# T sums of h in a second lane, z of the first half through DRAM, hi a unit ahead of lo

## The chip, the cores and the metric

The kernel runs on one core of one Trainium2 chip. The metric is the device time of one launch in microseconds. The median of three runs is 2718.05 us (2717.44 to 2718.52).

## What is computed

One residual block over 528 tokens (16 meta tokens and 512 of the sequence) of 2048 channels, in float32:

```
h = RMSNorm_pre(r);  z = h @ W_in + b_in      -> q, k, v, forget logits, pool input, two gates
m = sigmoid(g_attn) * (attention @ W_attn_o) + sigmoid(g_pool) * (pool @ W_pool_o)
r = r + RMSNorm_post(m @ W_out)
h = RMSNorm_pre(r)
a = causal_conv3(h @ W_up);  gate, val = split(a)          (11264 columns, 5632 each)
r = r + RMSNorm_post((gelu(gate) * val) @ W_down)
```

## The kernel before

**Layout and splitting.** Channels lie on the 128 partitions and tokens along the free axis. Every float32 product is made of three TensorE products of reduced-precision parts: each operand is split into hi (a cast by ScalarE, ACT) and lo (operand minus hi, by VectorE, DVE), and hi*hi, hi*lo and lo*hi are summed in PSUM.

**Weights.** They come from HBM in half tiles of 128x1024 ("units"), the loads on SP's queue. `load_next` fills `wraw` (six buffers), `convert_next` makes `whi` (L214, ACT) and then at once `wlo` (L215, DVE) in four buffers each. `weights` serves a tile of two units: when a tile begins it has the conversions up to two units past its own first two written out, and one more from its second half. Everything is issued in one order written out by hand: an engine executes its instructions in the order in which the Python emits them.

**Side work.** `Side` holds generators. `mm3` emits the matmuls of one k block and then calls `side.tick` with the time they are credited with (3 x 258 columns / 2330 = 0.332 for a half of the tokens). A generator that has yielded a number continues when that much was credited. `side.finish` emits all that is left at once.

**The stretch that the change touches.** The tokens are cut into two halves of 258 (with an overlap of two). The mixer's output projection (`mixer_out`, tile `pw`) first finishes half 0, then runs 12 tiles for half 1, about 1141 to 1215 us. Beside these 12 tiles goes `mixer_norm` of half 0. It reads the sum of squares (`rstd_from`: a matmul into `ps_rs`, then DVE and ACT steps, ending in the inverse root). Its first loop scales the projection (L814, DVE), adds the old residual (L818, POOL, with x loaded three steps ahead), stores it, squares it (L824, ACT) and adds up the squares (L816, DVE and POOL in turn); a second `rstd_from`; its second loop then makes h (L834, DVE), its hi (L836, ACT), stores h to DRAM and, one step later, makes its lo (L831, DVE). The numbers 2.2 and 2.0 (half 0), 1.8 and 1.5 (half 1) are the yields of the two loops. Then come the first six channel tiles of W_up for gate and value, once for half 0 and once for half 1 (`up_half`, tile `pu`, 12 tiles each); beside those of half 0 goes `mixer_norm` of half 1.

**Strassen-like pairs.** The other 38 channel tiles (`up_pair`) take seven products of 24 matmuls each in place of eight, over sums of weight blocks (S1 to S4, DVE) and sums of h blocks (T1 to T4). `sums_of_h` loads h from DRAM and makes the T's for each of eight k blocks: four DVE sums, two ACT casts, two DVE subtractions (L863 to L873). It is put into `side` when the second half phase starts, `combine` of a finished channel tile (convolution, gelu, product) is put ahead of it, and a `side.finish` ahead of the pairs emits what is left. In a pair, PSUM partial sums are copied by ACT to a `snap` tile (L914), and DVE adds a PSUM bank to that into `z`. All tiles of class F (activations) share 62 slots.

Of the kernel before, what the change touches and what calls it, by code (L numbers as in the profile page):

```python
# [32 lines left out]
LOOK = 3  # L33
# [19 lines left out]
EPS = 1e-6  # L53
NF = 62
NSP = 10
# [17 lines left out]
def block(ctx, tc, xT, win, wf, wao, wpw, wpo, wout, wup, wdn, consts, out):  # L73
# [50 lines left out]
    order += [("out", i) for i, _ in out_steps]  # L124
    NH = 6
    ups = lambda f0, f1: [("up", s * FT + f) for f in range(f0, f1) for s in (0, 1)]
    order += ups(0, NH) * 2
# [10 lines left out]
    for key in order:  # L138
# [10 lines left out]
    raws, ready, sums = {}, {}, {}  # L149
    at = {"load": 0, "conv": 0, "use": 0, "live": 0}  # L150
    NU = len(units)
# [24 lines left out]

    def unit_source(kind, n):

        if kind == "":
            return raw_of(n), lambda: drop(n)  # L180
        a11, a12, a21, a22 = (raw_of(n + i) for i in range(4))
        if kind == "11":
            return a11, lambda: None
        if kind == "12":
            return a12, lambda: None
        if kind == "22":
            return a22, lambda: drop(n + 3)
        if kind == "S3":
            def done():
                drop(n + 2)  # L190
                dve.tensor_tensor(a12, a12, sums["s2"], op=OP.subtract)
            return a21, done
        if kind == "S4":
            return a12, lambda: drop(n + 1)
        if kind == "S1":
            def done():
                dve.tensor_tensor(a21, a11, a21, op=OP.subtract)
                drop(n)
            return sums["s1"], done

        s1, s2 = (wp.tile([P, 1024], F32, name="wsum", tag="wsum", bufs=2) for _ in range(2))
        sums.update(s1=s1, s2=s2)
        dve.tensor_tensor(s1, a21, a22, op=OP.add)
        dve.tensor_tensor(s2, s1, a11, op=OP.subtract)  # L204
        return s2, lambda: None

    def convert_next(copy=act.copy):
        n = at["conv"]
        if n < NU - 8:
            kind, first = units[n]  # L210
            raw, done = unit_source(kind, first)
            hi = wp.tile([P, 1024], F32R, name="whi", tag="whi", bufs=HI)
            lo = wp.tile([P, 1024], F32R, name="wlo", tag="wlo", bufs=LO)
            copy(hi, raw)  # L214
            dve.tensor_tensor(lo, raw, f32(hi), op=OP.subtract)  # L215
            ready[n] = (hi, lo)
            done()
            at["conv"] += 1

    def prepare(n):  # L220
        while at["conv"] < min(NU - 8, n):
            convert_next()

    def weights(*key, ahead=1):

        n = at["use"]
        assert order[n] == key, (order[n], key)
        at["use"] += 1
        u = base[n]
        prepare(u + 2 + (2 if ahead else -1))  # L230
        if ahead:
            load_ahead()
        def w(t):
            if t >= 8 and ahead:
                prepare(u + 5)
                load_ahead()
            c = P * (t % 8)
            hi, lo = ready[u + t // 8]
            return hi[:, c:c + P], lo[:, c:c + P]
        return w  # L240

    def pair_weights(f):

        n = at["use"]
        assert order[n] == ("pair", f), (order[n], f)
        at["use"] += 1
        u = base[n]
        def unit(i):
            prepare(u + i + 1 + LOOK)
            load_ahead()  # L250
            hi, lo = ready[u + i]
            return lambda k: (hi[:, P * k:P * (k + 1)], lo[:, P * k:P * (k + 1)])
        return unit
# [41 lines left out]

    side = Side()

# [4 lines left out]
    def mm3(parts, nk, w, x, more=False):  # L302

        us = sum(3 * (xs.stop - xs.start) / 2330.0 for _, xs in parts)
        for k in range(nk):
            wh, wl = w(k)
            xh, xl = x(k)
            for j, (a, b) in enumerate(((wh, xh), (wh, xl), (wl, xh))):
                for po, xs in parts:
                    pe.matmul(po, a, b[:, xs], start=k == 0 and j == 0 and not more,  # L310
                              stop=k == nk - 1 and j == 2, skip_group_check=more)
            side.tick(us)


# [61 lines left out]
    for k in range(KT):  # L376
# [26 lines left out]
        if k == 7:  # L403
            convert_next()
    for k in range(KT - 3, KT):
# [359 lines left out]
    h_dram = dp.tile([2, KT, P, NA], F32, name="h_dram")  # L765
    act_dram = dp.tile([FT, P, SEQ], F32, name="act_dram")
    hb = [[], []]

# [3 lines left out]
    def mixer_out(i, es):  # L772
# [8 lines left out]
        for e, ps in zip(es, pss):  # L781
            if mix[e][i] is None:
                both = F("mix", n=2 * NA)
                mix[e][i & ~1], mix[e][i | 1] = both[:, :NA], both[:, NA:]
            act.copy(mix[e][i], ps)
            sq = F("sq2", n=NA)
# [6 lines left out]
    def mixer_norm(e, mix, acc, pace, pace2):  # L793
# [59 lines left out]

    def sums_of_h():

        for k in range(HK):
# [8 lines left out]
            h13, l13 = F("h13", F32R, 2 * NA), F("l13", F32R, 2 * NA)  # L865
# [3 lines left out]
            h24, l24 = F("h24", F32R, 2 * NA), F("l24", F32R, 2 * NA)  # L869
            act.copy(h24, t24)  # L870
            yield 1.5
            dve.tensor_tensor(l13, t13, f32(h13), op=OP.subtract)
            dve.tensor_tensor(l24, t24, f32(h24), op=OP.subtract)  # L873
            for name, h, l, j in (("T1", h13, l13, 0), ("T3", h13, l13, 1), ("T2", h24, l24, 0), ("T4", h24, l24, 1)):
                ts[name, k] = h[:, NA * j:NA * (j + 1)], l[:, NA * j:NA * (j + 1)]
            yield 1.5
# [28 lines left out]

    def up_half(e, m, z):
# [5 lines left out]
    def snap(src):  # L912
        t = sp.tile([P, NA], F32, name="snap", tag="snap", bufs=4)
        act.copy(t, src)  # L914
        return t

    def up_pair(f, late=None):
# [5 lines left out]
        def product(i, ps, block, more=False):  # L923
            mm3([(ps, slice(0, NA))], HK, unit(i), BLOCKS[block], more)

        product(0, a, "11")
# [12 lines left out]
        product(6, a, "T4", True)  # L939
        dve.tensor_tensor(zg[:, NA:NT], u2[:, 2:], c[:, 2:], op=OP.add)  # L940
        act.copy(zv[:, :NA], a)
        side.add(combine(zg, zv, f))

    zs = {}
    for e in range(2):
        if e == 1:
            side.finish()
            side.add(sums_of_h())
        for f in range(NH):
            for m in (f, FT + f):  # L950
                if e == 0:
                    zs[m] = F("z")
                up_half(e, m, zs[m])
            if e == 1:
                done = combine(zs.pop(f), zs.pop(FT + f), f)
                side.gens.insert(0, done) if side.gens else side.add(done)
    side.finish()

# [173 lines left out]
```

## Time and profile before

| | |
|---|---|
| median of three runs | 2718.05 us |
| the profiled execution | 2717.18 us, span 2715.4 us |
| mean granted TensorE clock | 0.983 |
| busy: PE, DVE, ACT, POOL | 97%, 61%, 38%, 5% of the span |

The profile page gives each engine's busy time, the span in 40 slices with the granted clock, the chain of waits that ended last and the costliest groups of instructions. Matmuls overlap in their pipeline, so PE's busy time alone doesn't tell its rate; the number of matmuls in a stretch does. PE is the TensorE matmul, PEld its weight load.

### The profile page before, as it was taken

The numbers are of one execution on the slowest core, as the hardware profiler recorded it, in microseconds if no ns is written. First come the engines' busy times: TensorE is split into PE (matmuls) and PEld (weight loads), VectorE is DVE, ScalarE is ACT, GpSimd is POOL, SyncE is SP. The second block draws the span as 40 slices with busy tenths as digits, with TensorE's granted clock in tenths as the row PEclk, the third lists the DMA queues.
The fourth block names the chain that finished last, engine by engine and source line by source line (L and its number), as shares of the span: only waits on it lengthen the run. The fifth ranks groups of instructions, "written<-read, shape, count | busy, mean of one in ns | idle before, by whom it ended". The sixth has DMA issues, their size and how long they took to land.

```text
span 2715.4 us, 46577 instructions
## 1 busy us (share of the span) xinstructions
PE 2622.0 (97%) x19669; PEld 2519.4 (93%) x19669; DVE 1652.6 (61%) x2144; ACT 1044.2 (38%) x1524; POOL 149.1 (5%) x204
## 2 busy tenths in 40 slices
PE   8999999999999999988969999999999999999995
PEld 8999999999999999988869999999999988888885
DVE  7655543223533334577688888888888845454557
ACT  4443342222232224444545455554554542222222
POOL 3000000000000000033000000000000000000003
PEclk9999999999999999998989999999999999999998
DMA  4322223332234323576643333333333343333323
GB/s 177 102 79 80 79 77 108 108 105 94 90 117 125 113 99 135 179 231 216 198 147 125 110 119 126 107 121 125 105 123 123 109 154 130 119 114 124 116 86 124
DMA packets 119377, 334.01 MB, mean 123 GB/s; under 512 B 13430, under 2 KB 38264, under 8 KB 119168
## 3 DMA queue, kind: packets, MB, share of 16 engines
q1 hardware_dynamic: 114944, 317.31, 35.4%
q0 software_dynamic: 4224, 13.72, 1.4%
q8 instruction: 154, 2.52, 0.4%
q14 instruction: 55, 0.45, 0.1%
HBM read 301.55 MB, written 29.43 MB: 122 GB/s over the span
## 4 chain that ended last, share of the span: by engine, by line
PE 89%; DVE 5%; issue 2%; ACT 2%; DMA 2%; POOL 0%; SPq 0%; DVEq 0%; ACTq 0%; POOLq 0%
PE pd L310 17%; PE pua L310 16%; PE puc L310 8%; PE pgp L310 7%; PE pga L310 7%; PE pw L310 6%; PE pu L310 6%; PE pub L310 4%; PE pv L310 3%; PE pao L310 3%; PE pk L310 3%; PE ppo L310 3%; PE pq L310 3%; ACT whi L214 1%; PE pa L589 1%
## 5 line engine op out<-in xcount | busy, mean ns | idle before, releaser
L215 DVE TENSOR_TENSOR wlo<-wraw,whi 128x1024 fp32r<-128x1024 f32 x536 | 659.4, 1232 | 417.5 <-ACT whi L214 416.9
L214 ACT CAST whi<-wraw 128x1024 fp32r<-128x1024 f32 x536 | 561.1, 1049 | 742.6 <-PE pd L310 227.9
L310 PE MATMUL pua<-h,whi 128*128 128x258 f32 x1520 | 370.2, 284 | 28.5 <-ACT snap L914 25.3
L310 PE MATMUL pua<-h,wlo 128*128 128x258 f32 x1216 | 345.6, 284 | 0.0
L310 PEld LDWEIGHTS pua<-h,whi 128*128 128x128 f32 x1520 | 267.6, 190 | 28.9 <-ACT snap L914 25.5
L310 PE MATMUL pua<-l,whi 128*128 128x258 f32 x912 | 259.1, 284 | 0.0
L310 PE MATMUL pd<-fh,wlo 128*128 128x512 f32 x640 | 252.2, 394 | 0.0
L310 PE MATMUL pd<-fh,whi 128*128 128x512 f32 x640 | 251.8, 393 | 0.0
L310 PE MATMUL pd<-fl,whi 128*128 128x512 f32 x640 | 251.7, 393 | 0.0
L310 PEld LDWEIGHTS pua<-h,wlo 128*128 128x128 f32 x1216 | 231.9, 191 | 0.0
L310 PE MATMUL puc<-h,whi 128*128 128x258 f32 x912 | 198.7, 284 | 0.0
L989 DVE TENSOR_TENSOR yacc<-yacc,pd 128x512 f32<-128x512 f32 x144 | 98.6, 685 | 145.1 <-PE pd L310 145.1
L310 PEld LDWEIGHTS pua<-l,whi 128*128 128x128 f32 x912 | 173.8, 191 | 0.0
L310 PE MATMUL puc<-h,wlo 128*128 128x258 f32 x608 | 172.4, 284 | 0.0
L310 PE MATMUL pu<-h,whi 128*128 128x258 f32 x768 | 149.9, 296 | 13.1 <-ACT sq L787 9.2
L310 PEld LDWEIGHTS puc<-h,whi 128*128 128x128 f32 x912 | 152.9, 190 | 0.0
L310 PEld LDWEIGHTS pd<-fl,whi 128*128 128x128 f32 x640 | 120.2, 188 | 28.2
L310 PEld LDWEIGHTS pd<-fh,wlo 128*128 128x128 f32 x640 | 120.2, 188 | 27.8
L310 PEld LDWEIGHTS pd<-fh,whi 128*128 128x128 f32 x640 | 120.2, 188 | 27.8
L310 PEld LDWEIGHTS pu<-h,whi 128*128 128x128 f32 x768 | 126.1, 200 | 16.0 <-ACT sq L787 9.4
L214 ACT CAST whi<-wsum 128x1024 fp32r<-128x1024 f32 x76 | 79.9, 1051 | 155.3 <-DVE wsum L204 155.3
L310 PE MATMUL pw<-ml,whi 128*128 128x258 f32 x512 | 136.1, 286 | 1.5 <-DVE ml L300 1.4
(316 smaller groups left out, 6109.1 us busy)
## 6 DMA issues: line engine op xcount, KB each, us to landing
wraw<-wup SPq DMA_DIRECT2D x200, 512.0 KB, 3.7
wraw<-win SPq DMA_DIRECT2D x128, 512.0 KB, 3.6
wraw<-wdn SPq DMA_DIRECT2D x88, 512.0 KB, 3.6
wraw<-wout SPq DMA_DIRECT2D x56, 512.0 KB, 3.9
act_dram<-cv POOLq DMA_DIRECT2D x44, 256.0 KB, 4.7
y<-act_dram SPq DMA_DIRECT2D x44, 256.0 KB, 4.9
wraw<-wao SPq DMA_DIRECT2D x16, 512.0 KB, 3.6
wraw<-wpo SPq DMA_DIRECT2D x16, 512.0 KB, 3.8
```

What stands on the lines that cost most here:

```text
L214: copy(hi, raw)
L215: dve.tensor_tensor(lo, raw, f32(hi), op=OP.subtract)
L310: pe.matmul(po, a, b[:, xs], start=k == 0 and j == 0 and not more, stop=k == nk - 1 and j == 2, skip_group_check=more)
L589: pe.matmul(pa[:, q0:], u, w[:, q0:], start=n == 0 and j == 0, stop=n == 4 and j == 2)
L989: dve.tensor_tensor(yacc[i], yacc[i], ps, op=OP.add)
```

## The change

- `NF` goes from 62 to 63 slots.
- The conversion of weights is cut into three steps with counters of their own: the sum or load (`make_source`), hi (`make_hi`) and lo (`make_lo`). In `weights`, lo is written out to one unit less far than before, hi one unit and sources two units ahead of lo. In pairs lo goes as far as before, hi isn't ahead, and a source is made right after the lo of the unit before it.
- `mixer_out` applies the post-norm's gain when it copies PSUM (an ACT activation with a scale); `mixer_norm` then multiplies by the inverse root alone. Its yields become 1.7 and 1.5 for both halves. In its second loop hi comes one step and lo two steps after h.
- `Side` exists twice; `mm3` ticks both. `sums_of_h` runs for k blocks 0 to 4 in the second lane beside `up_half` of half 1; blocks 5 to 7 are emitted after that phase, at once, ahead of the first pair. `combine` of the last half-phase tile is no longer finished ahead of the pairs.
- z of half 0 goes through DRAM: a POOL-issued store in the first half phase and an SP-issued load in the second, in place of 12 F tiles that stayed.
- In pairs, partial sums are copied by ACT straight into z and DVE adds in place; one ACT copy more per pair (`vr`).

```diff
-NF = 62
+NF = 63
...
+    def make_hi():
+        i = at["hi"]
+        while at["sum"] <= i:
+            make_source()
+        ready[i] = [wp.tile([P, 1024], F32R, name="whi", tag="whi", bufs=HI)]
+        act.copy(ready[i][0], sources[i])
+        at["hi"] += 1
+
+    def make_lo():
+        i = at["lo"]
+        while at["hi"] <= i:
+            make_hi()
+        lo = wp.tile([P, 1024], F32R, name="wlo", tag="wlo", bufs=LO)
+        dve.tensor_tensor(lo, sources.pop(i), f32(ready[i][0]), op=OP.subtract)
...
+    def prepare(n, ahead=1, ahead2=None):
+        n = min(n, NU - 8)
+        while at["lo"] < n:
+            make_lo()
+            for step, d, make in (("sum", 2 * ahead if ahead2 is None else ahead2, make_source), ("hi", ahead, make_hi)):
+                if at[step] < min(at["lo"] + d, NU - 8):
+                    make()
...
-        prepare(u + 2 + (2 if ahead else -1))
+        prepare(u + (LOOK if ahead else 1), ahead)
...
-                prepare(u + 5)
+                prepare(u + 1 + LOOK)
...
-            prepare(u + i + 1 + LOOK)
+            prepare(u + i + 1 + LOOK, 0, 1)
...
-    side = Side()
+    side, side2 = Side(), Side()
...
             side.tick(us)
+            side2.tick(us)
...
-            act.copy(mix[e][i], ps)
+            act.activation(mix[e][i], ps, AF.Identity, scale=col(C_G[1] + i))
...
-                dve.scalar_tensor_tensor(t, t, col(C_G[1] + i), rs1, op0=OP.mult, op1=OP.mult)
+                dve.tensor_tensor(t, t, rs1, op=OP.mult)
...
-        for i in range(KT + 1):
+        for i in range(KT + 2):
             yield pace2
-            if i:
-                hl = hb[e][i - 1]
-                dve.tensor_tensor(hl[:, NA:], mix[i - 1], f32(hl[:, :NA]), op=OP.subtract)
+            if i > 1:
+                hl = hb[e][i - 2]
+                dve.tensor_tensor(hl[:, NA:], mix[i - 2], f32(hl[:, :NA]), op=OP.subtract)
             if i < KT:
                 t = mix[i]
                 dve.scalar_tensor_tensor(t, t, col(C_G[2] + i), rs2, op0=OP.mult, op1=OP.mult)
+            if 1 <= i <= KT:
                 hl = F("h2", F32R, 2 * NA)
-                act.copy(hl[:, :NA], t)
-                nc.sync.dma_start(h_dram[e, i], t)
+                act.copy(hl[:, :NA], mix[i - 1])
+                nc.sync.dma_start(h_dram[e, i - 1], mix[i - 1])
                 hb[e].append(hl)
...
-            side.add(mixer_norm(0, mix[0], macc[0], 2.2, 2.0))
+            side.add(mixer_norm(0, mix[0], macc[0], 1.7, 1.5))
     side.finish()
-    side.add(mixer_norm(1, mix[1], macc[1], 1.8, 1.5))
+    side.add(mixer_norm(1, mix[1], macc[1], 1.7, 1.5))
...
-            yield 4.0
+            yield 3.0
...
+        z = F("z") if e else F("z0", n=NA)
+        if e:
+            nc.sync.dma_start(z[:, :NA], z_dram[n])
         mm3([(ps, slice(0, NA))], KT, w, lambda k: h_block(e, k))
-        act.copy(z[:, NA * e:NT], ps[:, 2 * e:]) if e else act.copy(z[:, :NA], ps)
+        if e:
+            act.copy(z[:, NA:NT], ps[:, 2:])
+        else:
+            act.copy(z, ps)
+            nc.gpsimd.dma_start(z_dram[n], z)
+        return z
...
         product(0, a, "11")
-        p1 = snap(a)
+        act.copy(gl, a)
         product(1, b, "21")
         product(2, a, "T2", True)
-        dve.tensor_tensor(zg[:, :NA], p1, b, op=OP.add)
-        u2 = snap(a)
+        act.copy(gr, a[:, 2:])
+        dve.tensor_tensor(gl, gl, b, op=OP.add)
         product(3, c, "T1")
-        p5 = snap(c)
+        act.copy(p5, c)
         product(4, a, "T3", True)
+        act.copy(vr, a[:, 2:])
         product(5, c, "22", True)
-        dve.tensor_tensor(zv[:, NA:NT], p5[:, 2:], a[:, 2:], op=OP.add)
+        dve.tensor_tensor(vr, vr, p5[:, 2:], op=OP.add)
         product(6, a, "T4", True)
...
         if e == 1:
             side.finish()
-            side.add(sums_of_h())
+            side2.add(sums_of_h(range(KE)))
...
-    side.finish()
+    side2.finish()
+    side2.add(sums_of_h(range(KE, HK)))
+    side2.finish()
```

## Rows read from the trace of the kernel before

**Rows 1.** The page: busy us, share of the span and instructions of each engine.
```profile
PE 2622.0 (97%) x19669; PEld 2519.4 (93%) x19669; DVE 1652.6 (61%) x2144; ACT 1044.2 (38%) x1524; POOL 149.1 (5%) x204
```
**Rows 2.** Busy time by stretch; after the stretch its length, x counts instructions.
```profile
core 0: us, PE busy (x) PEld busy (x) DVE busy (x) ACT busy (x) POOL busy (x), PEclk, DMA share, GB/s
...
1190.00:1200.00 10.00, 8.07 (x54) 7.84 (x53) 8.33 (x12) 4.09 (x10) 1.37 (x1) 0.83 0.67 230
...
1215.10:1240.00 24.90, 14.84 (x84) 13.35 (x83) 16.26 (x30) 10.80 (x22) 0.00 (x0) 0.73 0.48 152
1240.00:1270.00 30.00, 30.00 (x251) 30.00 (x250) 24.25 (x32) 13.88 (x26) 18.19 (x19) 1.00 0.87 272
1270.00:1285.00 15.00, 10.38 (x62) 9.77 (x62) 11.99 (x16) 7.21 (x12) 4.12 (x5) 0.77 0.67 213
1285.00:1325.00 40.00, 34.39 (x252) 32.42 (x251) 23.40 (x41) 16.97 (x30) 0.00 (x0) 0.94 0.54 172
1325.00:1335.00 10.00, 9.27 (x69) 9.06 (x68) 4.39 (x8) 4.40 (x7) 0.00 (x0) 0.89 0.48 159
1335.00:1389.80 54.80, 54.80 (x454) 54.80 (x453) 40.64 (x43) 32.70 (x44) 0.00 (x0) 1.00 0.66 216
...
1396.00:1421.00 25.00, 0.11 (x1) 0.11 (x1) 23.34 (x48) 9.92 (x16) 3.04 (x6) 0.56 0.39 127
1421.00:1441.00 20.00, 20.00 (x148) 20.00 (x149) 14.84 (x16) 9.06 (x12) 0.00 (x0) 0.87 0.32 106
1455.30:2143.10 687.80, 687.80 (x5714) 687.80 (x5713) 590.16 (x647) 349.21 (x476) 18.39 (x34) 1.00 0.35 118
```
**Rows 3.** PE's waits, 1130 to 1445 us: total us, times, longest.
```profile
PE pua L310 <- ACT snap L914: 25.3, 1, 25.3
```
**Rows 4.** PE's waits, 1421 to 2190 us.
```profile
PE pua L310 <- DVE z L938: 3.2, 1, 3.2
```
**Rows 5.** DVE in order of time, second loops: start, length, operation, [idle before <- releaser].
```profile
1231.40 0.43 DVE L831 TENSOR_TENSOR h<-mix,h 128x258 fp32r<-128x258 f32 x1 [0.47 <-ACT h L836]
...
1232.69 0.43 DVE L831 TENSOR_TENSOR h<-mix,h 128x258 fp32r<-128x258 f32 x1 [0.47 <-ACT h L836]
...
1315.08 1.23 DVE L215 TENSOR_TENSOR wlo<-wraw,whi 128x1024 fp32r<-128x1024 f32 x1 [1.69 <-ACT whi L214]
1316.22 0.42 DVE L831 TENSOR_TENSOR h<-mix,h 128x258 fp32r<-128x258 f32 x1
1316.56 0.48 DVE L834 SCALAR_TENSOR_TENSOR mix<-mix,cs,rs 128x258 f32<-128x258 f32 x1
```
**Rows 6.** DVE in order of time, the first loop of half 1.
```profile
1246.51 0.48 DVE L814 SCALAR_TENSOR_TENSOR mix<-mix,cs,rs 128x258 f32<-128x258 f32 x1
...
1273.64 0.95 DVE L814 SCALAR_TENSOR_TENSOR mix<-mix,cs,rs 128x258 f32<-128x258 f32 x1
```
**Rows 7.** Groups of DVE, 1242.4 to 1277.5 us: busy us, mean ns, idle before.
```profile
L215 DVE TENSOR_TENSOR wlo<-wraw,whi 128x1024 fp32r<-128x1024 f32 x13 | 17.1, 1312 | 7.4 <-ACT whi L214 7.4
```
**Rows 8.** POOL in order of time, the first loop of half 1.
```profile
1253.73 1.72 POOL L816 TENSOR_TENSOR acc<-acc,sq 128x258 f32<-128x258 f32 x1
...
1274.67 0.76 POOL L818 TENSOR_TENSOR mix<-mix,x 128x258 f32<-128x258 f32 x1 [0.36 <-DVE mix L814]
```
**Rows 9.** DMA issues, 1130 to 1430 us: count, KB each, median us to landing.
```profile
x<-xT SPq DMA_DIRECT2D x32, 129.0 KB, 5.0
```
**Rows 10.** DVE in order of time around the end of the half phases.
```profile
1387.78 1.23 DVE L204 TENSOR_TENSOR wsum<-wsum,wraw 128x1024 f32<-128x1024 f32 x1
...
1398.40 0.42 DVE L863 TENSOR_TENSOR t<-t 128x258 f32<-128x258 f32 x1
...
1401.50 0.42 DVE L863 TENSOR_TENSOR t<-t 128x258 f32<-128x258 f32 x1
```
**Rows 11.** ACT in order of time, in a pair.
```profile
1533.24 1.05 ACT L214 CAST whi<-wraw 128x1024 fp32r<-128x1024 f32 x1 [1.47 <-issue]
```
**Rows 12.** Groups of POOL, whole span: count, busy us, mean ns, idle before.
```profile
L903 POOL DMA_DIRECT2D act_dram<-cv x44 | 23.8, 542 | 897.8 <-DVE cv L902 897.6
```

More of the change, by code (lines that the diff above doesn't have):

```diff
@@ L125, in block @@
     NH = 6
+    KE = 5
     ups = lambda f0, f1: [("up", s * FT + f) for f in range(f0, f1) for s in (0, 1)]
@@ L148, in block @@
                 loads.append((srcs[key[0]](*key[1:]), c))
-    raws, ready, sums = {}, {}, {}
-    at = {"load": 0, "conv": 0, "use": 0, "live": 0}
+    raws, sources, ready, sums = {}, {}, {}, {}
+    at = {"load": 0, "sum": 0, "hi": 0, "lo": 0, "use": 0, "live": 0}
     NU = len(units)
@@ L175, in load_ahead, with make_source @@
             load_next()
-    def unit_source(kind, n):
+    def make_source():
+        i = at["sum"]
+        kind, n = units[i]
         if kind == "":
[L180 to L196, printed above, removed]
+            sources[i] = raw_of(n)
+        else:
+            a11, a12, a21, a22 = (raw_of(n + j) for j in range(4))
+            if kind == "S2":
+                for name in ("S1", "S2"):
+                    sums[name] = wp.tile([P, 1024], F32, name="wsum", tag="wsum", bufs=2)
+                dve.tensor_tensor(sums["S1"], a21, a22, op=OP.add)
+                dve.tensor_tensor(sums["S2"], sums["S1"], a11, op=OP.subtract)
+            elif kind == "S3":
@@ L197, in done @@
                 dve.tensor_tensor(a21, a11, a21, op=OP.subtract)
                 drop(n)
[L199 to L218, printed above, removed]
@@ L220, in prepare @@
-    def prepare(n):
-        while at["conv"] < min(NU - 8, n):
-            convert_next()
+            elif kind == "S4":
+                dve.tensor_tensor(a12, a12, sums["S2"], op=OP.subtract)
+            sources[i] = {"11": a11, "12": a12, "S3": a21, "S4": a12, "22": a22}.get(kind) or sums[kind]
+        at["sum"] += 1
+    def make_hi():
[5 more added lines that the diff above has]
+        at["hi"] += 1
@@ new lines, in make_lo @@
+    def make_lo():
[4 more added lines that the diff above has]
+        dve.tensor_tensor(lo, sources.pop(i), f32(ready[i][0]), op=OP.subtract)
+        ready[i].append(lo)
+        kind, n = units[i]
+        last = {"": 0, "S3": 2, "S4": 1, "22": 3}.get(kind)
+        if last is not None:
+            drop(n + last)
+        at["lo"] += 1
+    def prepare(n, ahead=1, ahead2=None):
[5 more added lines that the diff above has]
+                    make()
@@ L403, in block @@
         if k == 7:
-            convert_next()
+            make_lo()
     for k in range(KT - 3, KT):
@@ L766, in block @@
     act_dram = dp.tile([FT, P, SEQ], F32, name="act_dram")
+    z_dram = dp.tile([2 * NH, P, NA], F32, name="z_dram")
     hb = [[], []]
@@ L852, in block, with sums_of_h @@
     ts = {}
-    def sums_of_h():
-        for k in range(HK):
+    def sums_of_h(ks):
+        for k in ks:
             t13, t24 = F("t13", n=2 * NA), F("t24", n=2 * NA)
@@ L868, in sums_of_h @@
             dve.tensor_tensor(b21, b21, b22, op=OP.subtract)
-            h24, l24 = F("h24", F32R, 2 * NA), F("l24", F32R, 2 * NA)
             act.copy(h24, t24)
[L871 to L875, printed above, removed]
+            yield 2.0
+            for names, h, t in ((("T1", "T3"), h13, t13), (("T2", "T4"), h24, t24)):
+                lo = F("lt", F32R, 2 * NA)
+                dve.tensor_tensor(lo, t, f32(h), op=OP.subtract)
+                for j, name in enumerate(names):
+                    ts[name, k] = h[:, NA * j:NA * (j + 1)], lo[:, NA * j:NA * (j + 1)]
             yield 1.5
@@ L904, in combine, with up_half @@
         yield 0.1
-    def up_half(e, m, z):
+    def up_half(e, n, m):
         w = weights("up", m)
         ps = s_ps("pu0")[:, :NA]
+        z = F("z") if e else F("z0", n=NA)
+        if e:
+            nc.sync.dma_start(z[:, :NA], z_dram[n])
         mm3([(ps, slice(0, NA))], KT, w, lambda k: h_block(e, k))
-        act.copy(z[:, NA * e:NT], ps[:, 2 * e:]) if e else act.copy(z[:, :NA], ps)
[L912 to L915, printed above, removed]
+        if e:
+            act.copy(z[:, NA:NT], ps[:, 2:])
+        else:
+            act.copy(z, ps)
+            nc.gpsimd.dma_start(z_dram[n], z)
+        return z
     def up_pair(f, late=None):
@@ L924, in product @@
             mm3([(ps, slice(0, NA))], HK, unit(i), BLOCKS[block], more)
+        gl, gr, vl, vr = zg[:, :NA], zg[:, NA:NT], zv[:, :NA], zv[:, NA:NT]
+        p5 = sp.tile([P, NA], F32, name="snap", tag="snap", bufs=2)
         product(0, a, "11")
-        p1 = snap(a)
+        act.copy(gl, a)
         product(1, b, "21")
@@ L931, in up_pair @@
         product(2, a, "T2", True)
-        dve.tensor_tensor(zg[:, :NA], p1, b, op=OP.add)
-        u2 = snap(a)
+        act.copy(gr, a[:, 2:])
+        dve.tensor_tensor(gl, gl, b, op=OP.add)
         product(3, c, "T1")
-        p5 = snap(c)
+        act.copy(p5, c)
         product(4, a, "T3", True)
+        act.copy(vr, a[:, 2:])
         product(5, c, "22", True)
-        dve.tensor_tensor(zv[:, NA:NT], p5[:, 2:], a[:, 2:], op=OP.add)
+        dve.tensor_tensor(vr, vr, p5[:, 2:], op=OP.add)
         product(6, a, "T4", True)
-        dve.tensor_tensor(zg[:, NA:NT], u2[:, 2:], c[:, 2:], op=OP.add)
-        act.copy(zv[:, :NA], a)
+        act.copy(vl, a)
+        dve.tensor_tensor(gr, gr, c[:, 2:], op=OP.add)
         side.add(combine(zg, zv, f))
-    zs = {}
     for e in range(2):
@@ L947, in block @@
             side.finish()
-            side.add(sums_of_h())
+            side2.add(sums_of_h(range(KE)))
         for f in range(NH):
[L950 to L953, printed above, removed]
+            zg, zv = (up_half(e, 2 * f + j, j * FT + f) for j in (0, 1))
             if e == 1:
-                done = combine(zs.pop(f), zs.pop(FT + f), f)
-                side.gens.insert(0, done) if side.gens else side.add(done)
-    side.finish()
+                side.add(combine(zg, zv, f))
+    side2.finish()
+    side2.add(sums_of_h(range(KE, HK)))
+    side2.finish()
     acts = [[] for _ in range(NG)]
```

2 lines of the change are left out of this document (1 added, 1 removed).

## The prediction

> **What bounds the kernel now.** First the engines' busy time on the page: PE 97%, DVE 61%, ACT 38% [rows 1]. So a change can only win where PE stands still or runs at the lower clock. Then PE's waits and the table by stretch, to find those places; last DVE, ACT and POOL in order of time there, to see why.
>
> PE's full rate is read from the pairs: 5714 matmuls in 687.8 us, 0.1204 us each, at clock 1.00 [rows 2]. Eight k blocks (24 matmuls, one unit of weights) take 2.89 us, a half-phase tile 5.78 us. A stretch loses its length less 0.1204 us per matmul, which counts stalls and low clock together. From [rows 2]:
>
> - 1190 to 1200 (second inverse root of half 0): 10.0 - 6.5 = 3.5
> - 1215.1 to 1240 (from the last projection tile to the half phase): 24.9 - 10.1 = 14.8
> - 1240 to 1270 (first loop of half 1): 251 matmuls, nothing lost
> - 1270 to 1285 (second inverse root of half 1): 15.0 - 7.5 = 7.5
> - 1285 to 1325 (second loop of half 1): 40.0 - 30.3 = 9.7
> - 1325 to 1335 (second half phase begins): 10.0 - 8.3 = 1.7
> - 1335 to 1389.8: nothing (0.1)
> - ahead of the third product of the first pair: one wait of 25.3 [rows 3], in the stretch from 1396 to 1421, and 20.0 - 17.8 = 2.2 after it at clock 0.87 [rows 2], together 27.5.
>
> With one wait of 3.2 in the last pair [rows 4] that is 68.1 us, 2.5% of the time. Elsewhere the change meets a PE that is full.
>
> **The change, part by part**, against the profiled execution's own 2717.2 us (0.9 under the median).
>
> *Second loop of mixer_norm.* At the flush ahead of the half phase a step takes 1.29 us: DVE makes h, waits 0.47 us for ACT's cast, makes lo [rows 5], and PE waits for h. Beside matmuls the same coupling costs more, since ACT's weight cast stands behind the cast of h: DVE idles 1.69 us for it [rows 5]. The change gives hi one step and lo two steps of distance, and lo of weights no longer waits for a hi issued just before. What is left is DVE's own time. A unit is credited with 8 x 0.332 = 2.66, so a pace of 1.5 puts 1.77 steps on it: 1.14 (lo of the weights, 1315.08 to 1316.22) + 1.77 x (0.34 + 0.48) = 2.59 of 2.89 us [rows 5]. It fits with 10% to spare. The 9.7 of half 1 become 1.5 (bounds 0 and 5, half of what is).
>
> *Pace of half 0.* Credited time for its side work is 12 x 16 x 0.332 = 63.8. Before, 4 + 18 x 2.2 + 2 + 17 x 2.0 = 79.6 was asked, and the rest was flushed into the 14.8; now 4 + 18 x 1.7 + 2 + 18 x 1.5 = 63.6, and it fits. PE takes h blocks in order, 0.36 us each, so DVE may be some 5 us late without a stall. But half 1's first inverse root follows and blocks DVE for some time. I take 3 of the 14.8 as staying (0 to 8, a little over half).
>
> *First loops.* Thirteen steps of half 1 took 1246.51 to 1273.64, 2.09 us each [rows 6], where its 1.8 asked for 1.8 x 2.89 / 2.66 = 1.96. Now both halves ask for 1.85. DVE idled 7.4 of these 35 us waiting for ACT's hi [rows 7], and this wait goes. Against that, DVE and POOL hinder each other (a POOL sum takes 0.76 us alone, 1.72 us beside a lo [rows 8]); x lands after 5.0 us [rows 9] and is now asked for 3 x 1.85 = 5.6 us ahead; and the DMA share was already 0.87 at the slower pace [rows 2]. Lateness ends as a PE wait, because the matmul into `ps_rs` stands in PE's queue. At 2.09 us a step 18 steps are 18 x 0.24 = 4.3 us late. So 3.5 (half 0, from 2.2 to 1.7 the greater step) and 7.5 become 6 each, bounds 0 and 10.
>
> *z through DRAM.* Twelve stores cost POOL 0.54 us each, by the like store of `combine` [rows 12], beside 5.78 us a tile. They stand in POOL's queue ahead of the next residual sums and wait for ACT's copy of PSUM; the residual sums are late anyway. Twelve loads on SP stand between weight loads. Price 0, inside the bounds above; if this cover is gone, 12 x 0.54 = 6.5.
>
> *T sums beside the second half phase.* A k block takes DVE 3.10 us (1398.40 to 1401.50) [rows 10]; the tail before is seven of them and a rest. Five now lie beside the phase, 15.5 us, where DVE was busy 40.6 of 54.8 [rows 2]: 14 idle. It nearly fits, but they ask for 5 x 6.5 = 32.5 credited, so they crowd into the first half of it. I put 1.5 on it (0 to 5), and 2 (0 to 5) on the beginning, 1.7 before, where DVE waits for the first load of h.
>
> The tail: from the start of the last unit (2.89 us before the phase's end) DVE has one lo of weights (1.14), two sums of weights (2 x 1.23 [rows 10]), three k blocks (9.3) and the lo of S2 (1.14): 14.0, so it is through 11.1 us after the phase's end. PE has two products for 5.8 of that. DVE's lateness of perhaps 1 us makes the wait 6.3. The clock's return took 2.2; I keep 1.5. Then `combine` of the last half-phase tile now stands in the first pair, with no lead in weights: 2. Together 10 for 27.5 (5 to 17: DVE a unit ahead of PE, or the loads of h late by a landing time and DVE by another unit).
>
> *Pairs.* One ACT copy more (the old `snap` copies are the like), ACT being busy 349 of 688 us [rows 2]; DVE's sums are as many. ACT waits 1.47 us once a pair without a releaser named [rows 11], which I read as its hi waiting for PE to free a buffer; so the chain of conversions has that much to spare. Price 0 (0 to some 0.3 for each of 38 if that cover is gone, 11). The wait of 3.2 for DVE's z in the last pair becomes one for an ACT copy; I keep 2 (0 to 3.2).
>
> *Other phases.* Lo one unit less far ahead: full-width units take twice 2.89 us, so two units are 11 us of cover. ACT's order barely changes. Price 0. Gain on the copy in `mixer_out`: same count, 0.
>
> Sum of what stays: 6 + 3 + 6 + 1.5 + 2 + 1.5 + 10 + 2 = 32. Of 68.1 that saves 36: 2717.2 - 36 = 2681 us. All low ends together leave 5 (2654), all high ends 63 and 11 in the pairs (2723); not all fall alike, so its own range is 2662 to 2698.
>
> **The rivals.**
>
> *First loops don't hold the pace (2699).* For: the 1.72 us and the DMA share. Of a unit's 1.56 steps DVE needs 1.14 + 1.56 x 0.48 + 0.78 x 0.42 + 0.21 = 2.4 and POOL 1.56 x 0.76 + 0.78 x 0.74 = 1.8 (unhindered lengths [rows 5 to 8], the adds as L831). If they excluded each other wholly, a unit of steps would take 4.2 us, a step 2.7, 18 steps 15 us late in each half, 9 over my 6: 2681 + 18 = 2699. Against: in half 1 the same sum is 3.8 us a unit, yet PE lost nothing in 1240 to 1270, with DVE busy 24.3 and POOL 18.2 of 30 us, 42.4 in all; they ran side by side for at least 12. The Trainium skill (SBUF - State Buffer, "Who interferes with whom") says that a DVE instruction with two SBUF inputs and a GpSimd instruction that reads SBUF exclude each other, the later blocking until the first is done; by that rule this rival's time holds, less what POOL's stretched lengths hide. The stretched 1.72 agrees with it. Chance 0.09.
>
> *The lane only moves the stall (2695).* If DVE's idle 14 us are too broken to use, the five k blocks lengthen the second half phase by 15.5 instead of 1.5: 2695. Against: DVE's waits there are for a hi issued just before it, and these go. Chance 0.05. With the first rival on top, 2713, no change: 0.04.
>
> *Slower: the pairs lose their cover (2735).* In pairs hi isn't ahead, and DVE is busy 590 of 688 us [rows 2]. If the new order of source, hi and lo makes the chain through ACT longer than its spare 1.47 us [rows 11], all 38 pairs pay, at every one of them. A chain longer by one unit's 2.89 costs (2.89 - 1.47) x 38 = 54: 2681 + 54 = 2735. It turns the sign from 1.47 + 36 / 38 = 2.4 us a pair. Against: the sums S1 and S2 come earlier than before, and lo goes as far ahead. Chance 0.06.
>
> **How the numbers follow.** Forecast 0.76, the others 0.09, 0.05, 0.04, 0.06. Two tenths of a per cent, 5.4 us, is about what a measurement of this kernel can tell from no change. Faster: 0.76 + 0.09 + 0.05 = 0.90; same 0.04; slower 0.06. The range goes from 2660, a little under the forecast's own, to 2704, past the first two rivals.
>
> **What would show it.** Right: no DVE wait of half a us per step in the second loop; half phase beginning within 3 us of the last projection tile; five T blocks beside the second half phase; PE's wait in the first pair 5 to 9 us instead of 25.3; pairs still 20.2 us. Wrong: waits at `ps_rs` of over 10 us, fewer than 24 matmuls in 2.9 us in the second half phase, or pairs above 20.4 us.

## The result, and the profile after

The changed kernel takes 2683.84 us (median of 4 runs, 2680.76 to 2685.48), the kernel before, on the same chip, 2718.28 us. The ratio is 0.9871 with a 95% interval of 0.9854 to 0.9888: 34 us faster. The prediction was 2681. The profiled execution took 2685.48 us, its span is 2683.8 us; before it was 2715.4, so the traces account for 31.6 us. Two launches among the experiments, one of 3447 us in experiment 7 and the profiled one of 9056 us in experiment 9, were disturbed and stand in no figure below, so experiment 9 has no trace to read.

The page's row of engines, after, beside [rows 1]:

```profile
PE 2612.9 (97%) x19669; PEld 2510.8 (94%) x19669; DVE 1638.1 (61%) x2144; ACT 1055.6 (39%) x1562; POOL 147.0 (5%) x216
```

PE has the same 19669 matmuls. ACT has 38 copies more, POOL 12 stores more. The work is as large as before; what changed is how long one engine stands for another. The starts and ends of PE's tiles, from the view of one tile of either trace (us), show where:

| from, to | before | after | difference |
|---|---|---|---|
| start to first gate matmul (`pga`) | 360.3 | 365.8 | +5.5 |
| to first projection matmul (`pw`) | 1022.3 | 1028.4 | +0.6 |
| to first half-phase matmul (`pu`) | 1224.5 | 1224.3 | -6.3 |
| to the first pair's third product | 1420.9 | 1394.0 | -26.7 |
| to first down matmul (`pd`) | 2191.3 | 2158.3 | -6.1 |
| to the end of the span | 2715.4 | 2683.8 | +1.4 |

The differences add up to -31.6. The first row is a loss that the prediction didn't have; its size varies, since six of the other kernels below have the same code up to there and start their gates at 363.1 to 365.0 us.

Busy time by stretch, after, beside [rows 2] (the same columns). A stretch loses its length less 0.1204 us per matmul:

```profile
60.00:80.00 20.00, 17.32 (x122) 17.11 (x121) 13.45 (x26) 10.74 (x14) 0.00 (x0) 0.83 0.21 67
1165.00:1200.00 35.00, 31.46 (x247) 29.95 (x246) 30.60 (x42) 18.15 (x36) 17.47 (x18) 1.00 0.80 258
...
1222.00:1230.00 8.00, 7.16 (x58) 6.89 (x57) 5.43 (x9) 4.40 (x8) 0.00 (x0) 1.00 0.97 297
1230.00:1258.00 28.00, 28.00 (x234) 28.00 (x233) 27.58 (x31) 13.65 (x24) 18.57 (x20) 1.00 0.86 285
1258.00:1270.00 12.00, 9.68 (x76) 9.21 (x75) 10.25 (x12) 7.28 (x14) 7.28 (x11) 1.00 0.87 275
1270.00:1300.00 30.00, 30.00 (x251) 30.00 (x250) 27.71 (x48) 17.29 (x32) 3.12 (x6) 1.00 0.92 281
1300.00:1312.00 12.00, 10.99 (x91) 10.78 (x91) 5.71 (x9) 4.46 (x6) 0.00 (x0) 1.00 0.55 177
1312.00:1350.00 38.00, 29.06 (x214) 28.00 (x214) 27.10 (x41) 19.45 (x29) 0.54 (x1) 0.91 0.65 203
1350.00:1380.50 30.50, 30.50 (x255) 30.50 (x254) 26.68 (x30) 17.58 (x25) 1.63 (x3) 1.00 0.84 264
1380.50:1404.00 23.50, 16.27 (x113) 16.06 (x113) 20.58 (x31) 13.21 (x20) 0.54 (x1) 0.78 0.34 105
1428.60:2116.40 687.80, 687.80 (x5725) 687.80 (x5724) 591.66 (x648) 358.69 (x510) 18.42 (x34) 1.00 0.34 118
2109.30:2158.30 49.00, 49.00 (x411) 49.00 (x410) 39.69 (x44) 25.53 (x37) 1.63 (x3) 1.00 0.45 152
```

Read the count against the length: 1270 to 1300 (second loop of half 1) holds 251 matmuls in 30.0 us, nothing lost, where 1285 to 1325 lost 9.7 before. In 1312 to 1350, beside the T sums, 214 matmuls would take 25.8 us: 12.2 are lost, the largest loss left. That is 16 matmuls in 2.9 us where full rate is 24, one of the prediction's own signs of being wrong. The pairs run at full rate, 5725 matmuls in the same 687.8 us. PE's waits, after (total us, times, longest), those of [rows 3, 4] and the two that bear on the change:

```profile
PE pu L314 <- DVE wlo L212: 10.3, 7, 4.7
PE pua L314 <- ACT z L940: 7.2, 1, 7.2
...
PE ps_rs L334 <- DVE acc L822: 4.0, 2, 2.0
```

The wait of 25.3 us in the first pair is 7.2; the wait of 3.2 in the last pair is gone. New is the first row: the second half phase stands 10.3 us for the lo of its weights.

### The profile page after: what moved, and what is told of

It reads as the page before. It is cut to its first block, busy times and chain, and to the rows that moved or that the text cites. A ratio compares the mean times of both kernels' runs of the same rounds, so it can differ in the third digit from the quotient of the medians.

```text
span 2683.8 us, 46625 instructions
## 1 busy us (share of the span) xinstructions
PE 2612.9 (97%) x19669; PEld 2510.8 (94%) x19669; DVE 1638.1 (61%) x2144; ACT 1055.6 (39%) x1562; POOL 147.0 (5%) x216
## 4 chain that ended last, share of the span: by engine, by line
PE 48%; DMA 2%; DVE 2%; issue 1%; POOL 1%; ACT 0%; SPq 0%; DVEq 0%; POOLq 0%; ACTq 0%
PE pd L314 18%; PE pua L314 16%; PE puc L314 8%; PE pub L314 4%; PE pu L314 1%; DMA t<-h_dram 1%; DMA z<-z_dram 1%; DMA x<-xT 0%; DVE wlo L212 0%; DMA y<-act_dram 0%; DVE yacc L1036 0%; POOL mix L824 0%; PE ps_rs L334 0%; DVE rs L338 0%; DMA wraw<-wup 0%
## 5 line engine op out<-in xcount | busy, mean ns | idle before, releaser
L314 PE MATMUL pua<-lt,whi 128*128 128x258 f32 x912 | 259.2, 284 | 0.0
L314 PEld LDWEIGHTS pua<-lt,whi 128*128 128x128 f32 x912 | 172.8, 190 | 0.0
L314 PE MATMUL pu<-h,whi 128*128 128x258 f32 x768 | 141.8, 287 | 0.8 <-ACT sq L793 0.8
L314 PE MATMUL pw<-mh,wlo 128*128 128x258 f32 x512 | 135.7, 285 | 2.9 <-DVE wlo L212 2.9
```

## The experiments

Each kernel is the changed kernel with one edit, unless said. "Gives back" means slower than the changed kernel by so much. All were timed beside the kernel before on the same chip, whose medians were 2716.9 to 2718.8; where two kernels lie within 2 us of each other, the ratios to it decide.

**1. Conversions as far ahead as before, outside the half phases.** The edit tells whether the 5.5 us ahead of the gates come from lo being a unit less far.

```
-        prepare(u + (LOOK if ahead else 1), ahead)
+        far = LOOK + (key[0] in ("in", "ao", "pw", "po"))
+        prepare(u + (far if ahead else 1), ahead if far == LOOK else 0, 2 if ahead and far > LOOK else None)
...
-                prepare(u + 1 + LOOK)
+                prepare(u + 1 + far, ahead if far == LOOK else 0, 2 if far > LOOK else None)
```

> The changed kernel, but in all tiles ahead of the output projection the conversions go as before: hi and lo to the same unit, lo one unit further. Theory (the shorter reach of lo costs the 5.5 us that PE lost between 60 and 80 us, where DVE stands behind the forget logits' ACT steps): that wait goes, the gates begin at 360 to 361 us instead of 365.8, and the time is 2677 to 2680. Rival (the early loss is a different start of the run, or comes of ACT): the gates begin at 365 or later and the time stays at 2683 to 2685.

Measured: 2681.81 us (2679.83 to 2683.11), ratio 0.9866 (0.9853 to 0.988). The stretch from 60 to 80 us in this kernel:

```profile
60.00:80.00 20.00, 20.00 (x169) 20.00 (x168) 12.79 (x24) 10.49 (x14) 0.00 (x0) 1.00 0.17 56
```

It is full again with 169 matmuls, where the changed kernel has 122, and the gates start at 360.4 us. Hi reaches as far as in the changed kernel, lo and the sources a unit further, so the cause of the early loss is shown. The time missed its range of 2677 to 2680: of the 6.2 us that the trace is ahead at the last projection matmul (1217.0 against 1223.2), 3.9 are left at the first down matmul (2154.4 against 2158.3), since the half phases gave 1.9 back. By the medians it is 2 us, with intervals that overlap.

**2. The loads of T one k block ahead.** It takes away DVE's wait for the loads and leaves its work.

```
         for k in ks:
-            t13, t24 = F("t13", n=2 * NA), F("t24", n=2 * NA)
...
+            t_load(k)
+            if k == 0:
+                yield 3.0
+            t_load(k + 1)
             yield 3.0
+            t13, t24 = t_in.pop(k)
```

> The changed kernel, but the loads of h for a T block are issued one block ahead (the first block waits 3.0 more credited us). Theory (the 13 us that PE lost from 1300 to 1350 come of DVE's queue standing behind loads that land late, 17.9 us of such waits): DVE's waits for these loads fall under 6 us, PE loses 3 to 6 us there, time 2673 to 2677. Rival (DVE has simply too much to do in this stretch, the T sums only moved): waits for loads fall, but PE still loses 10 or more there, time 2681 to 2685.

Measured: 2670.39 us (2668.53 to 2673.58), ratio 0.9825 (0.9811 to 0.9838): 13 us faster than the changed kernel and 3 better than the range expected. DVE's waits for these loads in the second half phase and the tail, in the changed kernel:

```profile
DVE t L870 <- DMA t<-h_dram: 17.9, 5, 5.8
```

in this kernel:

```profile
DVE t L878 <- DMA t<-h_dram: 3.0, 1, 3.0
```

and here PE's wait and the whole stretch beside the T sums:

```profile
PE pu L314 <- DVE wlo L212: 0.3, 1, 0.3
```

```profile
1300.00:1368.40 68.40, 68.13 (x565) 67.92 (x564) 60.20 (x81) 42.08 (x59) 2.17 (x4) 1.00 0.85 275
```

565 matmuls at 0.1204 are 68.0 of 68.4 us, where 3 to 6 us of loss were expected to stay. DVE is busy 60.2 us of them and PE loses nothing: not DVE's load but its waits held PE.

**3. The T sums in the one lane, as before.**

```
-            side2.add(sums_of_h(range(KE)))
+            side.add(sums_of_h(range(HK)))
...
-                side.add(combine(zg, zv, f))
-    side2.finish()
-    side2.add(sums_of_h(range(KE, HK)))
-    side2.finish()
+                done = combine(zg, zv, f)
+                side.gens.insert(0, done) if side.gens else side.add(done)
+    side.finish()
```

> The changed kernel with the T sums back in the one lane: all eight blocks behind the combines, the rest emitted at once ahead of the pairs. Theory (the lane took 17.7 us from the tail and gave 11 to 12 back in the second half phase): the wait ahead of the third product is 22 to 26 us again, the second half phase loses 1 to 3 us, time 2688 to 2694. Rival (the loss in the second half phase is not the lane's, but the z loads' and the shorter reach of lo): that phase still loses 10 or more, time 2699 to 2704.

Measured: 2692.89 us (2692.4 to 2693.98), ratio 0.9908 (0.9895 to 0.9922). PE's wait in the first pair:

```profile
PE pua L314 <- ACT z L940: 23.6, 1, 23.6
```

The lane gains 16.4 us at that wait and gives about half back in the half phases, which take 147.8 us here (1223.5 to 1371.3) and 156.5 in the changed kernel: 9 us net by the medians. The z loads still run in this kernel, so they alone are not what the changed kernel loses there.

**4. The old conversion** (`convert_next` and `unit_source` in place of the three steps for sum, hi and lo; all else of the change).

> The changed kernel with the old conversion of weights (source, hi and lo of a unit together, lo one unit further). Theory (the distance in the second loop and the paces pay only if lo doesn't wait for a hi issued just before it): early loss gone (-5.5), but the loops beside half phase and projection lose 10 to 20 more, time 2688 to 2700. Rival (the split of hi and lo is worth nothing by itself; what pays is the order in the loops): time 2676 to 2682.

Measured: 2705.32 us (2702.55 to 2706.49), ratio 0.9952 (0.9939 to 0.9966). It gives back 21 us, above the 4 to 16 expected (2688 to 2700), and that although it has no early loss (its projection starts at 1023 us). DVE's wait for ACT's hi, 1230 to 1385 us, in this kernel:

```profile
DVE wlo L217 <- ACT whi L216: 29.5, 20, 4.1
```

In the changed kernel, same stretch:

```profile
DVE wlo L212 <- ACT whi L204: 1.6, 2, 1.4
```

PE's waits in the old conversion that are longer than in the changed kernel:

```profile
PE pua L312 <- ACT z L938: 12.0, 1, 12.0
PE ps_rs L332 <- DVE acc L820: 9.8, 2, 5.6
PE pu L312 <- ACT whi L216: 8.8, 4, 3.7
PE pu L312 <- ACT sq L791: 4.0, 1, 4.0
```

So the new order of conversion, hi a unit ahead of lo, is the largest part of the gain among those taken away one at a time, and it acts in projection, half phases and tail at once. (The edit also takes back the earlier sources and lo's shorter reach, which it can't tell apart from hi.)

**5. The old paces** (2.2 and 2.0 for half 0, 1.8 and 1.5 for half 1).

> The changed kernel with the old yields of the norm loops (2.2 and 2.0, 1.8 and 1.5). Theory (half 0's work fits beside its 12 tiles only at 1.7 and 1.5): some nine steps of the second loop are flushed ahead of the half phase again, 0.8 to 0.9 us each now instead of 1.29, so PE loses 6 to 9 us more between projection and half phase, the waits at the inverse roots shrink by 1 to 2, time 2688 to 2692. Rival (DVE, not the pace, sets how far the loops get): 2682 to 2686.

Measured: 2684.85 us (2683.1 to 2687.81), ratio 0.9882 (0.9868 to 0.9895): no difference, as the rival had it. At the old pace 1190 to 1200 us runs full, 81 matmuls, and the boundary of 1215 to 1240 loses 25.0 - 185 x 0.1204 = 2.7. So in the new order of steps the old pace doesn't bring the 14.8 us of before back.

**6. The old pairs** (partial sums through `snap`, three buffers where the kernel before had four, DVE adding from PSUM).

> The changed kernel with the pairs' partial sums as before (snap tiles, DVE adding two of them into z, no copy of vr). Theory (the copy into z pays once, in the last pair, where PE lost 5.3 us by a wait for DVE's sum; elsewhere both are free): the wait of about 3 us in the last pair is back, pairs still 20.23 us, time 2687 to 2690. Rival (that wait is gone for another reason, the order of the conversions): 2682 to 2685.

Measured: 2823.02 us (2820.22 to 2826.51), ratio 1.039 (1.0376 to 1.0404). Both theories were wrong by 130 us. PE now waits in every pair:

```profile
PE pua L314 <- DVE z L954: 83.0, 38, 3.1
```

Experiment 10 takes the cause apart.

**7. The old second loop of `mixer_norm`** (hi and lo of h in one step's distance less: `KT + 1` steps, the cast in the step that makes h).

> The changed kernel with hi in the step of h and lo one step later in the second loop, as before. Theory (each step again makes ACT's queue wait for DVE's h, with the weights' hi behind it): DVE waits about half a us for the cast of h in most of 34 steps, PE loses 5 to 12 us more in and after the second loops, time 2689 to 2696. Rival (lo of weights no longer waiting for its hi is enough, DVE has the slack): 2682 to 2686.

Measured: 2695.4 us (2695.0 to 2696.26), ratio 0.992 (0.9905 to 0.9935), as expected: it gives back 12 us. PE's first half-phase tile starts at 1231.1, 5.0 us after the last projection matmul, against 1.1; the rest is lost in the projection (199.2 us for 194.8) and the half phases (161.3 for 156.5).

**8. Experiments 1 and 2 together.**

> The changed kernel with both: conversions as before ahead of the output projection, and the loads of h for the T sums a block ahead. Theory (two separate places, the first giving 2 to 5.4 us, the second 13.4): 2665 to 2668. Rival (the early gain is used up at a later wait that doesn't move): 2669 to 2671.

Measured: 2668.53 us (2666.64 to 2669.17), ratio 0.9819 (0.9806 to 0.9833). It adds 2 us to experiment 2, as experiment 1 did to the changed kernel; here too the intervals overlap.

**9. All sums of squares of the first loops on POOL** (on top of 8; it tests whether DVE or POOL sets the first loops).

```
-                (dve if i % 2 else pool).tensor_tensor(acc2, acc2, sqs[i - 2], op=OP.add)
+                pool.tensor_tensor(acc2, acc2, sqs[i - 2], op=OP.add)
```

> The kernel with both additions (conversions as before ahead of the projection, T loads a block ahead), and in the first loops all sums of squares on POOL instead of every second one on DVE. Theory (in the first loops DVE is the late engine, POOL waits for it): 0.3 us less for DVE per unit, the waits of PE at the inverse roots fall from 4.0 to 2 to 3 us in all, time 2665 to 2668. Rival (DVE and POOL exclude each other, so moving a sum gains nothing, and POOL's 0.74 us are slower than DVE's 0.34): the waits grow to 5 to 9, time 2670 to 2676.

Measured: 2676.63 us (2676.32 to 2677.99), ratio 0.9847 (0.9834 to 0.986): 8 us slower than experiment 8, nearest to the rival's range. Where the 8 us are lost isn't shown, for only the times are known.

**10. The changed kernel without the copy of the right half of value** (`vr`); DVE adds it from PSUM instead.

```
-        act.copy(vr, a[:, 2:])
...
-        dve.tensor_tensor(vr, vr, p5[:, 2:], op=OP.add)
+        dve.tensor_tensor(vr, p5[:, 2:], a[:, 2:], op=OP.add)
```

> The changed kernel without the one added ACT copy per pair: DVE adds the PSUM bank of T3 and the T1 copy into z as before; two snap buffers as in the changed kernel. Theory (the conversions now put both sums of S1 and S2, 2.45 us, ahead of that add in DVE's queue, and PE's seventh product waits for it, so the copy is what pays for the new order): 38 waits of about 2 us for DVE's z in the pairs, with a lower clock after each, time 2810 to 2830. Rival (the pairs suffered for want of snap buffers): no such wait, 2684 to 2690.

Measured: 2825.75 us (2819.13 to 2827.02), ratio 1.039 (1.0375 to 1.0404), as the theory had it: one copy in each of 38 pairs is worth 142 us. DVE in order of time in a pair, in this kernel (start, length, operation):

```profile
1501.85 1.22 DVE L189 TENSOR_TENSOR wsum<-wraw 128x1024 f32<-128x1024 f32 x1
1503.10 1.22 DVE L190 TENSOR_TENSOR wsum<-wsum,wraw 128x1024 f32<-128x1024 f32 x1
1504.24 0.41 DVE L951 TENSOR_TENSOR z<-snap,pua 128x256 f32<-128x256 f32 x1
...
1528.37 0.41 DVE L951 TENSOR_TENSOR z<-snap,pua 128x256 f32<-128x256 f32 x1
```

and in the kernel before:

```profile
1515.22 0.41 DVE L938 TENSOR_TENSOR z<-snap,pua 128x256 f32<-128x256 f32 x1
1515.55 1.22 DVE L203 TENSOR_TENSOR wsum<-wraw 128x1024 f32<-128x1024 f32 x1
1516.80 1.23 DVE L204 TENSOR_TENSOR wsum<-wsum,wraw 128x1024 f32<-128x1024 f32 x1
```

Before, the add that frees `pua` stood ahead of the two sums of weights; now the sums are made a unit earlier and stand ahead of it. PE waits for the add:

```profile
1504.71 0.40 PE L314 MATMUL pua<-h,whi 128*128 128x258 f32 x1 [2.16 <-DVE z L951]
...
1528.84 0.40 PE L314 MATMUL pua<-h,whi 128*128 128x258 f32 x1 [2.15 <-DVE z L951]
```

A pair takes 24.1 us (1528.37 - 1504.24) for 20.2: 2.2 of standing, and 1.7 more after it at the lower clock, whose mean is 0.93 in this pair.

**11. Two of the four sums of the last three T blocks on POOL** (on top of 8).

```
+            eng = pool if k >= KE else dve
-            dve.tensor_tensor(b11, b12, b11, op=OP.subtract)
-            dve.tensor_tensor(b12, b22, b12, op=OP.subtract)
+            eng.tensor_tensor(b11, b12, b11, op=OP.subtract)
+            eng.tensor_tensor(b12, b22, b12, op=OP.subtract)
```

> The kernel with both additions, and for the three T blocks after the half phases the first two of four sums on POOL. Theory (the tail is DVE's 3 x 3.1 us in a row): DVE's time per block falls to 2.3 us, PE's wait ahead of the third product from 5.6 to 3 to 4 us, time 2665 to 2667. Rival (the four sums are one dependent chain, and POOL's are slower, 0.76 for 0.46 us, and in DVE's way): wait 5.5 to 8, time 2668 to 2671.

Measured: 2664.74 us (2664.29 to 2667.07), ratio 0.9804 (0.9791 to 0.9817); PE's wait in the first pair is 4.0 us, where experiment 8 has 5.6. So DVE's own time set at least part of the tail.

**12. All sums of squares on DVE** (on top of 11, the reverse of 9).

> The kernel with both additions and two tail sums on POOL, and in the first loops all sums of squares on DVE. Theory (moving DVE's to POOL cost 8 us, so POOL, at 0.74 us against 0.34, is what makes these loops late; the other way gives something back): waits at the inverse roots fall from 4.4 to 2 to 3 us, time 2660 to 2663. Rival (DVE is as full, 64 of 70 us busy, and both directions lose): waits 4 to 7, time 2665 to 2669.

Measured: 2662.76 us (2661.76 to 2663.91), ratio 0.98 (0.9787 to 0.9814). The ratio is that of experiment 11 within 0.0004, 1 us, and the intervals nearly coincide, so no gain of this edit is shown (the medians differ by 2 us, but so do those of the kernel before on the two chips). Either version is about 20 us under the changed kernel. What PE still waits for around the change:

```profile
PE pua L315 <- ACT z L950: 3.8, 1, 3.8
PE ps_rs L335 <- DVE acc L823: 3.6, 2, 2.3
```

Not tested by itself: z through DRAM, the 63rd slot, and the gain applied in the copy of `mixer_out`. Taken away singly, the lane, the conversions and the second loop cost 9, 21 and 12 us, together more than the 34 gained, so these parts overlap.

## Why the prediction was right, and where its terms were not

The prediction named the place (PE's losses between 1190 and 1421 us) and the mechanism (DVE and ACT waiting for each other ahead of PE), and the time came out 3 us above it. That it came so near is in part luck: two terms were too small by 15 us together, others too large by almost 10. Its terms, by the windows above:

| what stays lost, us | before | predicted | measured |
|---|---|---|---|
| first loop of half 0 (35.0 - 247 x 0.1204) | 3.5 | 6 | 5.3 |
| boundary to the half phase | 14.8 | 3 | 1.0 |
| first loop of half 1 (1230 to 1270) | 7.5 | 6 | 2.7 |
| second loop of half 1 | 9.7 | 1.5 | 0 |
| second half phase: begin, and beside the T blocks | 1.7 | 2 + 1.5 | 1.0 + 12.2 |
| tail, with the clock after it | 27.5 | 10 | 9.9 |
| last pair (4.8 before with the clock: 49.0 - 367 x 0.1204, 2142.3 to 2191.3) | 3.2 | 2 | 0 |
| other phases | 0 | 0 | 5.6 |
| sum | 68 | 32 | 37.7 |

**The step that was mis-sized is "T sums beside the second half phase": 3.5 forecast, 13.2 measured.** The arithmetic of DVE's work held: experiment 2 puts the same sums into the same phase at PE's full rate. What failed is the step from "14 us idle" to "it nearly fits". The sums are in DVE's one queue with the lo of the weights, and their loads were asked for 3.0 credited us ahead. The price of a late load stood in the prediction only for the first block and in the tail's bounds. DVE in order of time, after:

```profile
1306.25 0.43 DVE L870 TENSOR_TENSOR t<-t 128x258 f32<-128x258 f32 x1 [5.83 <-DMA t<-h_dram]
...
1309.37 2.35 DVE L212 TENSOR_TENSOR wlo<-wraw,whi 128x1024 fp32r<-128x1024 f32 x2
1315.81 0.43 DVE L870 TENSOR_TENSOR t<-t 128x258 f32<-128x258 f32 x1 [4.09 <-DMA t<-h_dram]
...
1336.10 0.43 DVE L870 TENSOR_TENSOR t<-t 128x258 f32<-128x258 f32 x1 [4.05 <-DMA t<-h_dram]
...
1339.28 1.22 DVE L212 TENSOR_TENSOR wlo<-wraw,whi 128x1024 fp32r<-128x1024 f32 x1
```

and PE:

```profile
1310.65 0.39 PE L314 MATMUL pu<-h,wlo 128*128 128x258 f32 x1 [1.01 <-DVE wlo L212]
...
1318.82 0.39 PE L314 MATMUL pu<-h,wlo 128*128 128x258 f32 x1 [2.13 <-DVE wlo L212]
...
1340.55 0.58 PE L314 MATMUL pu<-h,wlo 128*128 128x258 f32 x1 [4.68 <-DVE wlo L212]
```

For 5.83, 4.09 and 4.05 us nothing behind the waiting subtraction moved, the lo of weights among it, and PE stood for that lo, longest (4.68 us) behind the last of them, where sums of T and two steps of `combine` stood ahead of it too. This is the rival "the lane only moves the stall" at most of its price, by another cause than the one it named: the 14 us of DVE that this rival called too broken to use were usable once the loads came earlier.

**"Other phases: price 0" was wrong by 5.6 us.** I counted cover in units of PE (two units, 11 us) and not in DVE's order. The lo of the input projection's weights stands behind the forget gate's chain, which waits for ACT. DVE, after:

```profile
67.18 0.42 DVE L436 TENSOR_SCALAR fb<-fa 8x528 f32<-8x528 f32 x1 [3.50 <-ACT fa L435]
69.14 0.42 DVE L439 TENSOR_SCALAR fb<-fb 8x528 f32<-8x528 f32 x1 [1.53 <-ACT fc L437]
...
71.68 1.21 DVE L212 TENSOR_TENSOR wlo<-wraw,whi 128x1024 fp32r<-128x1024 f32 x1
```

PE stood 2.7 us for it; at the lower clock after that the stretch lost (169 - 122) x 0.1184 = 5.6 (0.1184 is 20 us by 169). With one unit more (experiment 1) nothing is lost there.

**Better than forecast.** The boundary, the first loop of half 1, the second loop and the last pair came out 8.8 us better than their terms, which makes up for most of the T term. For the boundary my reason was partly wrong: I put it on the pace that fits the credited time, and the pace is worth nothing (experiment 5). What it hung on is the order of hi and lo: from the last projection matmul to the half phase PE needs 1.1 us, 4.3 with the old order in the weights (experiment 4) and 5.0 with the old order in h (experiment 7). In the first loop of half 1 DVE's wait for hi of weights went from 7.4 us to none, as predicted, and the steps took 1.93 us (15 from 1234.52 to 1263.43), faster than the 2.09 of before though not the 1.85 asked.

**The tail** was right to 0.1 us in sum, by luck in part, for it was divided otherwise: a wait of 7.2 and 2.7 beside it, for 6.3, 1.5 and 2.

**The pairs: price 0 was right, for a reason that I hadn't seen.** The prediction took the added copy for a cost to be covered. It is what keeps the slower rival away. That rival ("the pairs lose their cover", sign at 2.4 us a pair) looked for its price in ACT's chain; the new order has it in DVE's, 3.9 us a pair, as soon as a DVE add from PSUM stands in it (experiments 6 and 10). My chance of 0.06 rested on the spare of ACT, and no row of mine looked at what stands ahead of the add on DVE.

**First rival (DVE and POOL).** Its physics was nearer than I allowed; its consequence did not come. DVE in order of time, after, in the first loop of half 1:

```profile
1253.11 2.85 DVE L212 TENSOR_TENSOR wlo<-wraw,whi 128x1024 fp32r<-128x1024 f32 x1
```

POOL at the same time:

```profile
1253.42 0.75 POOL L822 TENSOR_TENSOR acc<-acc,sq 128x258 f32<-128x258 f32 x1
1254.13 0.74 POOL L824 TENSOR_TENSOR mix<-mix,x 128x258 f32<-128x258 f32 x1
```

A lo of 1.21 us alone lasts 2.85: 1.21 + 0.75 + 0.74 = 2.70, so the whole of both POOL operations fits in it. My counter, that DVE and POOL together were busy 42.4 of 30 us and so ran side by side, doesn't hold, since a recorded length, as this one shows, can include time blocked. (A term of my sum for this rival, 0.21 us of DVE a unit, names no row.) The Trainium skill (SBUF - State Buffer, "Who interferes with whom") calls the shared port an exclusive lock. These rows agree in that the lo lasts longer by about what POOL works; they don't show that whoever comes first keeps the port, for both POOL sums begin after the lo (by 0.31 and 1.02 us) and are not stretched. The time of that rival, 2699, still wasn't reached: the first loops lost 8.0 us together, against the 12 that I gave them and the 18 more of the rival. The rival supposed that the sums exclude each other for all of a step; in 1230 to 1258 DVE was busy 27.58 of 28 us with blocked time in it, and PE still ran full.

What stays open: why experiment 1 brings 2 us in the medians where 5.6 us of stall went. Two parts are seen: 1.9 us were given back in the half phases, and the profiled execution of the changed kernel had the latest gates of all (365.8 us; 363.1 to 365.0 in the other kernels with that code), so its early loss is above the usual one.

## What to carry to other kernels

When work is moved beside a full engine, don't only sum its time: go through the queue that it joins, and for each instruction in it that can wait (for a load, for another engine's cast) ask who stands behind; a load asked for one block earlier was worth 13 us here, without any work less. An engine's order is part of a buffer's release: two sums of 1.2 us that slipped ahead of one short add that frees PSUM cost 142 us in 38 pairs, and one copy on an engine with time to spare took it away. And an engine pair that exchanges halves of a result (cast here, subtract there) wants the first half a unit ahead: that was the largest part of this change.

## What the runs showed of the hardware

- The longer waits of PE cost more than their length: 2.7 us at 72 us became 5.6, 2.2 in a pair of experiment 10 became 3.9 (mean granted clock of the pair 0.93), 7.2 in the first pair 9.9. After the wait of 7.2 us in the first pair, matmuls of 258 columns start 0.21 us apart (1394.58, 1394.79), the lower of the two clock levels, 1.2 GHz, against 0.12 at the pairs' full rate; 61 run in 10 us where 83 would.

```profile
1394.00:1404.00 10.00, 10.00 (x61) 10.00 (x62) 9.74 (x12) 5.14 (x7) 0.54 (x1) 0.70 0.49 154
```

```profile
1393.98 0.58 PE L314 MATMUL pua<-h,whi 128*128 128x258 f32 x1 [7.23 <-ACT z L940]
...
1394.58 0.42 PE L314 MATMUL pua<-h,wlo 128*128 128x258 f32 x1
1394.79 0.42 PE L314 MATMUL pua<-h,whi 128*128 128x258 f32 x1
```

- Some transfers landed later in the changed kernel, where more moved at once (mean 238 GB/s from 1130 to 1390 us, 196 before from 1130 to 1430). The 129 KB loads of T took 3.4 us (median) before and 4.4 after, the stores of h 3.4 and 5.8, with z beside them; the loads of x of the same size stayed at 5.0 and 5.1. Why some and not others isn't shown. After:

```profile
h_dram<-mix SPq DMA_DIRECT2D x32, 129.0 KB, 5.8
t<-h_dram SPq DMA_DIRECT2D x32, 129.0 KB, 4.4
```

- A POOL sum of 128x258 takes 0.75 us and, by the rows above, holds a DVE lo up for about that time; on DVE the same sum is 0.41. Moving DVE's half of these sums to POOL cost 8 us (experiment 9); moving POOL's half to DVE made no difference that the runs can tell (experiment 12).
